# The feed-forwards' matrix products by one level of Strassen's algorithm, with sums of weight blocks made on chip

## The chip, the cores and the metric

The kernel runs on one core of a Trainium2 chip. The core has five engines with a queue each, which wait for one another by semaphores: TensorE (PE in the profile; its weight loads are PEld), VectorE (DVE), ScalarE (ACT), GpSimd (POOL) and SyncE (SP, which issues most transfers). The metric is the time of one execution on the device in microseconds (us), the median of several runs.

## The reference, cut to what matters

The program is a chain of three transformer-like layers on 512 tokens of 1024 features in float32: a gated recurrence, a dilated attention, and a block of sparse attention beside linear attention. Each is followed by a norm and a gated feed-forward of inner width 2816. The change touches the three feed-forwards alone.

```python
def rmsnorm(x, gain):
    xf = x.astype(jnp.float32)
    y = xf * lax.rsqrt(jnp.mean(xf * xf, axis=-1, keepdims=True) + NORM_EPS)
    return (y * gain.astype(jnp.float32)).astype(x.dtype)

def swiglu_ffn(u, w_in, w_down):                 # [512, 1024], [1024, 5632], [2816, 1024]
    gate, up = jnp.split(u @ w_in, 2, axis=-1)
    return (jax.nn.silu(gate) * up) @ w_down

    # first_block, per layer; second block likewise with w_ffn_gate, w_ffn_up, w_ffn_down
    h = h + mix
    h = h + swiglu_ffn(rmsnorm(h, norm_ffn[layer]), ffn_w_in[layer], ffn_w_down[layer])
```

## The kernel before

Activations lie feature-major: a tile is 128 features by 512 tokens. A product of 128 x 128 weights with such a tile is done in three passes (mm3): each operand is split into a head, rounded to the type that PE reads at full pace (fp32r), and a rest, and rest times head, head times head and head times rest are summed in a PSUM bank. So one block of weights costs three matmuls of 512 columns.

The class Weights streams the weights in the order of use. A unit is 1024 columns, that is eight blocks. SP loads it (w_raw, three buffers), ACT casts it to the head (w_hi), and DVE for even units, POOL for odd ones, subtracts the head from the raw weights (w_lo, the rest). `take` hands out blocks; after 3/8 of a unit it has the heads of up to three units made, after 5/8 the rests. Nothing else decides the order there: each engine runs its instructions in the order in which this code issues them, and a tile that is not there makes the whole queue of its reader wait.

A feed-forward (ffn) runs in two halves of 11 inner tiles. For each inner tile, gemm makes the gate and the up product over 8 blocks each (evac_up: DVE scales the gate by the norm's factor r_bc, ACT applies silu, POOL multiplies by r_bc, DVE multiplies with the up product, then h is split into its parts by ACT and DVE). Then the half's 8 output tiles are made over 11 blocks each and added to the residual x (evac_dn), in the second half with the operands and squares of the next norm (norm_feed). The first operands u are x times the gain, split; the norm's factor is applied after the product, since it is known only two tiles later. In the last feed-forward, finish makes the last output tile in two halves of the tokens, so that the first half can be normed and stored under the second.

All operations are recorded by a wrapper, so nearly every row of the profile has line L228; in the changed kernel that line is L263. Rows are told apart by the names of their tiles: ps is a PSUM bank, u and h are the operands' parts.

Of the kernel before, what the change touches and what calls it, by code (L numbers as in the profile page):

```python
# [17 lines left out]
KD = 8  # L18
FF = 22
FH = 11  # L20
# [4 lines left out]
# columns of the packed per-feature vectors  # L25
# [10 lines left out]
# columns of the constants that stay  # L36
# [16 lines left out]
def nsa_rows():  # L53
    """Feature order of the NSA heads: tile j holds head j of group 0 and head j of group 1."""
    return np.concatenate([np.arange((e * 4 + j) * 64, (e * 4 + j) * 64 + 64) for j in range(4) for e in range(2)])


def attn_heads():
    """(head of the group, group) in the order in which the output projection takes them."""
    return [(t, g) for t in range(4) for g in (1, 2)] + [(t, 0) for t in range(4)]  # L60


def weight_plan():
    """The order in which weight blocks are used: (section, [(matrix, k tile, columns)])."""
# [14 lines left out]
    def ffn(name_in, name_down, name_up=None):  # L79
        out = []  # L80
        for half in range(2):
            tiles = []
            for i in range(FH):
                tiles.append(cols((half * FH + i) * 128))
                tiles.append(cols(FF * 128 + (half * FH + i) * 128))
            out += fm(name_in, range(KD), tiles, 2 if half == 0 else 1)
            out += fm(name_down, range(half * FH, half * FH + FH), [cols(m * 128) for m in range(8)], 2)
        return out
# [9 lines left out]
    plan.append(("hgrn", c))  # L98
# [8 lines left out]
    plan.append(("attn", c))  # L107
# [26 lines left out]
    plan.append(("blk2", c))  # L134
    plan.append(("ffn2", ffn("fin2", "fdn2")))
# [3 lines left out]
def plan_units(sec, chunks):  # L139
    """Cut a section's blocks into units of at most UNIT columns; the first ones are small, to start early."""  # L140
# [171 lines left out]
class Program:  # L312
# [1144 lines left out]
    def finish(self, hh):  # L1457
# [41 lines left out]
        for k in range(FH):  # L1499
            product(0, k)  # L1500
# [151 lines left out]
```

## Time and profile before

| | |
|---|---|
| median of 3 runs | 2164.24 us (2163.97 to 2165.24) |
| profiled execution: span from first to last instruction | 2162.1 us |
| PE busy | 2117.4 us, 98% |
| DVE, ACT, POOL busy | 1004.3, 783.8, 723.6 us |
| weights read, mean rate over the span | 187.25 MB read from HBM, 88 GB/s |
| mean granted PE clock | 0.994 |

The profiled execution has no time of its own beside its span; the median of the runs is 2.1 us above that. Busy times are unions over the span; a matmul's recorded duration includes its way through the array, so the pace is read from the distance between starts. The engines beside PE are less busy, but each stage has its own share, so stages are read in windows.

### The profile page before, as it was taken

How to read it: one execution, taken by the hardware profiler on the slowest of the kernel's cores; microseconds unless marked ns; L12 is line 12 of the kernel's file. 1: busy time of each engine (PE TensorE's matmuls, PEld its weight loads, DVE VectorE, ACT ScalarE, POOL GpSimd, SP SyncE). 2: the span in 40 equal slices, each digit the busy share in tenths (PEclk: the TensorE clock that was granted, in tenths of full speed). 3: DMA queues.
4: the chain of work that ended last, by engine and by line, in shares of the span. 5: the costliest groups of instructions: out<-in, count | busy, mean ns of one | idle time of the engine just before them, and what ended most of it. 6: DMA issues, size and time to landing. Idle time of an engine off the chain costs nothing.

```text
span 2162.1 us, 25412 instructions
## 1 busy us (share of the span) xinstructions
PE 2117.4 (98%) x9983; PEld 1773.4 (82%) x9983; DVE 1004.3 (46%) x1775; ACT 783.8 (36%) x1290; POOL 723.6 (33%) x442
## 2 busy tenths in 40 slices
PE   9999999999999999999999999999899999999998
PEld 7787788888888998788888888887688788888887
DVE  4778853322334555643322333447778753222322
ACT  5343443222233433443222224244455543222233
POOL 4413343323333434323322335331511253322333
PEclk9999999999999999999999999999999999999999
DMA  5111233323323222222332232321111223333332
GB/s 178 59 59 49 69 127 98 98 98 98 98 88 107 79 88 78 79 69 98 98 102 93 98 98 92 133 69 48 55 55 57 70 95 98 98 98 98 96 100 69
DMA packets 55865, 191.00 MB, mean 88 GB/s; under 512 B 6257, under 2 KB 8321, under 8 KB 55745
## 3 DMA queue, kind: packets, MB, share of 16 engines
q1 hardware_dynamic: 53584, 183.85, 26.2%
q0 software_dynamic: 1008, 3.42, 0.4%
q10 hardware_dynamic: 1152, 2.10, 0.3%
q8 instruction: 78, 1.28, 0.2%
q14 instruction: 43, 0.34, 0.1%
HBM read 187.25 MB, written 2.10 MB: 88 GB/s over the span
## 4 chain that ended last, share of the span: by engine, by line
PE 86%; DVE 9%; issue 1%; POOL 1%; ACT 1%; DMA 1%; SPq 0%; DVEq 0%; ACTq 0%; POOLq 0%
PE ps L228 86%; DVE Q L228 2%; DVE Sd L228 2%; DVE P L228 1%; DMA w_raw<-in_hgrn 1%; DVE w_lo L228 1%; DVE K L228 0%; POOL rot L228 0%; DVE Pc L228 0%; DVE qs L228 0%; POOL rs L228 0%; DVE obl L228 0%; DVE GQ L228 0%; DVE PT L228 0%; POOL w_lo L228 0%
## 5 line engine op out<-in xcount | busy, mean ns | idle before, releaser
L228 PE MATMUL ps<-u,w_hi 128*128 128x512 f32 x3392 | 1049.4, 391 | 0.0
L228 PEld LDWEIGHTS ps<-u,w_hi 128*128 128x128 f32 x3392 | 638.9, 188 | 128.9 <-issue 1.4
L228 PE MATMUL ps<-u,w_lo 128*128 128x512 f32 x1696 | 683.7, 403 | 2.2 <-POOL w_lo L228 2.2
L228 POOL TENSOR_TENSOR w_lo<-w_raw,w_hi 128x1024 fp32r<-128x1024 f32 (+2 forms) x173 | 415.8, 2403 | 745.1 <-ACT w_hi L228 636.2
L228 ACT CAST w_hi<-w_raw 128x1024 fp32r<-128x1024 f32 (+2 forms) x346 | 356.1, 1030 | 301.6 <-PE ps L228 205.4
L228 PEld LDWEIGHTS ps<-u,w_lo 128*128 128x128 f32 x1696 | 319.7, 189 | 68.3 <-issue 4.2
L228 PE MATMUL ps<-h,w_hi 128*128 128x512 f32 (+1 forms) x1078 | 326.3, 385 | 0.0
L228 DVE TENSOR_TENSOR w_lo<-w_raw,w_hi 128x1024 fp32r<-128x1024 f32 (+2 forms) x173 | 231.5, 1338 | 183.7 <-ACT w_hi L228 175.4
L228 PEld LDWEIGHTS ps<-h,w_hi 128*128 128x128 f32 x1078 | 200.9, 188 | 40.4
L228 PE MATMUL ps<-h,w_lo 128*128 128x512 f32 (+1 forms) x539 | 207.6, 385 | 0.5 <-DVE x L228 0.5
L228 POOL TENSOR_TENSOR sg<-sg,r_bc 128x512 f32<-128x512 f32 x66 | 85.8, 1299 | 290.3 <-ACT sg L228 290.3
L228 DVE TENSOR_TENSOR x<-x,ps 128x512 f32<-128x512 f32 (+1 forms) x73 | 49.5, 678 | 218.6 <-PE ps L228 218.6
L228 PE MATMUL ps<-w_hi,u 128*128 128x512 f32 (+1 forms) x448 | 139.1, 392 | 2.3 <-DVE u L228 2.3
L228 DVE TENSOR_TENSOR h<-ps,sg 128x512 f32<-128x512 f32 x66 | 45.7, 692 | 194.9 <-PE ps L228 182.4
L228 ACT ACTIVATE sg<-gs 128x512 f32<-128x512 f32 x66 | 41.7, 632 | 242.3 <-DVE gs L228 242.3
L228 ACT CAST h<-h 128x512 fp32r<-128x512 f32 x66 | 41.0, 620 | 242.8 <-DVE h L228 242.8
L228 DVE TENSOR_TENSOR gs<-ps,r_bc 128x512 f32<-128x512 f32 x66 | 45.6, 691 | 156.8 <-PE ps L228 156.7
L228 PEld LDWEIGHTS ps<-h,w_lo 128*128 128x128 f32 x539 | 101.2, 188 | 20.9 <-DVE x L228 0.7
L228 ACT ACTIVATE P<-P,nm 128x128 f32<-128x128 f32 (+2 forms) x112 | 55.2, 494 | 142.6 <-DVE nm L228 130.4
L228 POOL TENSOR_TENSOR sq_acc<-sq_acc,sq 128x512 f32<-128x512 f32 x48 | 67.2, 1405 | 117.8 <-ACT sq L228 115.7
L228 PEld LDWEIGHTS ps<-w_hi,u 128*128 128x128 f32 x448 | 95.0, 226 | 10.3 <-DVE u L228 2.7
L228 PE MATMUL ps<-w_lo,u 128*128 128x512 f32 (+1 forms) x224 | 85.8, 383 | 0.0
(294 smaller groups left out, 2231.5 us busy)
## 6 DMA issues: line engine op xcount, KB each, us to landing
w_raw<-in_ffn SPq DMA_DIRECT2D x198, 512.0 KB, 3.5
w_raw<-in_attn SPq DMA_DIRECT2D x48, 512.0 KB, 3.5
w_raw<-in_blk SPq DMA_DIRECT2D x47, 512.0 KB, 3.4
w_raw<-in_hgrn SPq DMA_DIRECT2D x36, 512.0 KB, 3.5
w_raw<-in_blk SPq DMA_DIRECT2D x7, 404.0 KB, 2.9
x<-in_xt SPq DMA_DIRECT2D x8, 256.0 KB, 5.1
w_raw<-in_hgrn SPq DMA_DIRECT2D x8, 256.0 KB, 4.0
x<-in_xt ACTq DMA_DIRECT2D x8, 256.0 KB, 5.0
```

The costliest lines, as they stand in the source:

```text
L228: r = f(*args, **kw)
```

## The change

Where the diff takes comments and docstrings away, nothing changes. What it does:

- **Strassen's form.** The product of a pair of weight tiles (gate and up tile of one inner index, or two output tiles) with an even number of inner blocks and 512 tokens is cut in two along each of the three dimensions. Seven products of half size replace eight; in the code they are a1, b1, a2, b2, c, a3, a4, which collect in three banks (a, b and c). Each product's matmuls have 256 columns; the inner dimension of a group is four pairs of blocks for up groups, three or two pairs for down groups. Each of the 22 inner tiles but the first four makes an up group, and the 11 pairs of inner tiles are worked off in chunks of 3, 3, 2 and 3, with four down groups each (three and a plain product in the last feed-forward).
- **Sums of weights.** Four of the seven products need sums of weight quarters. POOL makes them (ws) from the raw tiles, ahead of the heads. Heads of the sums and the raw quarters are cast by ACT in halves of a unit; in this part all rests (w_lo) are made by DVE.
- **Sums of operands.** The norm's factor must be in the operands now, so the normed operands are made anew (normed) beside plain tiles 4 to 7 of the first four inner tiles; POOL makes their sums, ACT the heads (P1, P2, P3), DVE the rests. The inner tiles h are treated in the same way in a4 of each up group: operands_1 for even ones, operands_2 for odd ones.
- **Evacuation.** Each product's part of a bank is evacuated by itself, 256 columns: by an ACT copy the first time, else by DVE additions or a multiplication; POOL multiplies the up half with the silu.
- **Buffers.** Four w_raw buffers, not three; 28 larger tiles, not 26.

By the program's order, matmuls of 512 columns go from 8059 to 3916 and those of 256 columns from 130 to 7381; the other forms stay.

```diff
+FC = 4
+FCHUNKS = [(0, 1, 2), (3, 4, 5), (6, 7), (8, 9, 10)]
+def ffn_jobs(last):
+    ks = [(2 * j, 2 * j + 1) for j in range(KD // 2)]
+    def ups(a, b):
+        return [("u", i, ks) for i in range(a, b)]
+    def downs(c, n=4):
+        return [("d", i, [(2 * q, 2 * q + 1) for q in FCHUNKS[c]]) for i in range(n)]
+    return ups(FC, 7) + downs(0) + ups(7, 13) + downs(1) + ups(13, FF) + downs(2) + downs(3, 3 if last else 4)
+S_AT = {"a1": 0, "b1": 1, "a2": 3, "b2": 4, "c": 5, "a3": 6, "a4": 9}
+S_LAST = {"a1": 0, "b1": 1, "a2": 3, "c": 4, "a3": 5, "b2": 6, "a4": 7}
+def strassen_order(n):
+    at = [(7 * g + t, g, p) for g in range(n) for p, t in (S_AT if g < n - 1 else S_LAST).items()]
+    return [(g, p) for _, g, p in sorted(at)]
...
+    RAW, SPLIT = 4, 3
...
+    def load(self, n):
+        while self.n_dma < min(n, len(self.raws)):
+            r = self.raws[self.n_dma]
+            r[3] = self.raw_p.tile([128, UNIT], F32, name="w_raw", tag="w_raw")
+            self.nc.sync.dma_start(r[3][:, :r[1]], r[0])
+            self.n_dma += 1
...
+    def used(self, i):
+        self.raws[i][2] -= 1
+        self.n_free += self.raws[i][2] == 0
...
+    def quarter(self, grp, q):
+        n = grp["n"]
+        r = self.raw(grp["r"][0 if q[1] == "1" and q != "A21" or q == "A12" else 1])
+        o = 0 if q in ("A11", "A22") else n
+        return r[:, o:o + n]
+    def sums(self, n):
+        while self.n_sum < min(n, len(self.units)):
+            for part in self.units[self.n_sum]:
+                if part[0] == "s" and part[2] in ("b1", "a2", "b2", "a3"):
+                    grp, p = part[1:]
+                    s = grp["s"][p] = self.s2("ws")[:, 0:grp["n"]]
+                    q, ss = (lambda name: self.quarter(grp, name)), grp["s"]
+                    if p == "b1":
+                        self.g.tensor_add(s, q("A21"), q("A22"))
+                    elif p == "a2":
+                        self.g.tensor_sub(s, ss["b1"], q("A11"))
+                    elif p == "b2":
+                        self.g.tensor_sub(s, q("A12"), ss["a2"])
+                    else:
+                        self.g.tensor_sub(s, q("A11"), q("A21"))
+                    for i in {"b1": (1,), "a2": (0,), "b2": (0,), "a3": (0, 1)}[p]:
+                        self.used(grp["r"][i])
+            self.n_sum += 1
+    def source(self, part):
+        if part[0] == "c":
+            return self.raw(part[1])[:, :self.raws[part[1]][1]]
+        grp, p = part[1:]
+        return self.quarter(grp, {"a1": "A11", "c": "A12", "a4": "A22"}[p]) if p in ("a1", "c", "a4") else grp["s"][p]
+    def width(self, part):
+        return self.raws[part[1]][1] if part[0] == "c" else part[1]["n"]
     def heads(self, look):
         while self.n_head < min(self.at + look, len(self.units)):
             u = self.n_head
-            self.load(u + 1)
-            w = self.units[u][2]
+            self.sums(u + 2)
             hi = self.sp_p.tile([128, UNIT], F32R, name="w_hi", tag="w_hi")
             lo = self.sp_p.tile([128, UNIT], F32R, name="w_lo", tag="w_lo")
-            self.a.copy(hi[:, :w], self.raw[u][:, :w])
+            o = 0
+            for part in self.units[u]:
+                w = self.width(part)
+                self.a.copy(hi[:, o:o + w], self.source(part))
+                o += w
             self.split[u] = (hi, lo)
             self.n_head += 1
     def rests(self):
         while self.n_rest < self.n_head:
-            u = self.n_rest
-            w = self.units[u][2]
+            u, o = self.n_rest, 0
             hi, lo = self.split[u]
-            (self.g if u % 2 else self.v).tensor_sub(lo[:, :w], self.raw.pop(u)[:, :w], hi[:, :w].bitcast(F32))
+            for part in self.units[u]:
+                w = self.width(part)
...
+                e = self.g if part[0] == "c" and u % 2 else self.v
+                e.tensor_sub(lo[:, o:o + w], self.source(part), hi[:, o:o + w].bitcast(F32))
+                o += w
+                if part[0] == "c":
+                    self.used(part[1])
+                elif part[2] in ("a1", "c", "a4"):
+                    self.used(part[1]["r"][part[2] == "a4"])
             self.n_rest += 1
-        self.load(self.n_rest + self.RAW - 1)
...
+    def product(self, p):
+        self.begin()
+        unit = self.units[self.at]
+        part = unit[self.idx]
+        assert part[0] == "s" and part[2] == p, (self.at, self.idx, part, p)
+        self.todo = (self.at, self.idx, len(unit))
+        return self.next(part[1]["n"], len(unit))
+    def prepare(self):
+        at, idx, n = self.todo
+        if idx == 0:
+            self.split_from(at)
+        if idx == n - 1:
+            self.rests()
+    def split_from(self, at):
+        now, self.at = self.at, at
+        self.heads(self.look)
+        self.at = now
...
+    def operands_1(self, E1, B12=False):
+        v, a, g = self.v, self.a, self.g
+        g.tensor_sub(E1[:, 2], E1[:, 1], E1[:, 0])
+        P = self.s4("P1", (128, 2, 2, 256), F32R)
+        a.copy(P[:, 0], E1[:, 0::2])
+        v.tensor_sub(P[:, 1], E1[:, 0::2], P[:, 0].bitcast(F32))
+        return {"a1": (P[:, 0, 0], P[:, 1, 0]), "b1": (P[:, 0, 1], P[:, 1, 1])}
+    def operands_2(self, E1, E2):
+        v, a, g = self.v, self.a, self.g
+        g.tensor_sub(E2[:, 2], E2[:, 1], E1[:, 2])
+        g.tensor_sub(E2[:, 3], E2[:, 0], E2[:, 2])
+        hi, lo = (self.s4("P2", (128, 4, 256), F32R) for _ in range(2))
+        a.copy(hi, E2)
+        v.tensor_sub(lo, E2, hi.bitcast(F32))
+        g.tensor_sub(E1[:, 3], E2[:, 1], E1[:, 1])
+        X = {p: (hi[:, i], lo[:, i]) for i, p in enumerate(("c", "b2", "a2", "a4"))}
+        X["a3"] = self.half(E1[:, 3], "P3")
+        return X
+    def half(self, src, name):
+        P = self.s2(name, (128, 2, 256), F32R)
+        self.a.copy(P[:, 0], src)
+        self.v.tensor_sub(P[:, 1], src, P[:, 0].bitcast(F32))
+        return P[:, 0], P[:, 1]
+    def strassen(self, groups):
+        banks = {}
+        for g, p in strassen_order(len(groups)):
+            operands, after = groups[g]
+            key = g, p[0]
+            first = key not in banks
+            if first:
+                banks[key] = self.ps((128, 256))
+            ps, X = banks[key], operands()
+            hi, lo = self.W.product(p)
+            for j in range(len(X)):
+                x, sl = X[j][p], slice(128 * j, 128 * j + 128)
+                self.mm3(ps, (hi[:, sl], lo[:, sl]), x, first and j == 0, j == len(X) - 1)
+            after[p](ps)
+            self.W.prepare()
...
     def ffn(self, gain_name, pre=None, gain=None, operands=True, residues=False):
         v, a, g = self.v, self.a, self.g
...
+        last = not operands
+        n1, n2 = slice(0, 256), slice(256, 512)
+        inner = self.V[self.ffn_gain]
+        E, H, U, sr = {}, {}, [], {}
+        def room(i):
+            if i not in E:
+                E[i] = self.s4("E", (128, 4, 256))
+            return E[i]
+        def normed(j):
+            e = [self.s4("E", (128, 4, 256)) for _ in range(2)]
+            for i in range(2):
+                k = 2 * j + i
+                v.scalar_tensor_tensor(
+                    e[i][:, 0:2].rearrange("p a n -> p (a n)"), self.x[k], inner[:, k:k + 1], self.r_bc, op0=ALU.mult, op1=ALU.mult)
+            X = self.operands_1(e[0])
+            X.update(self.operands_2(*e))
+            U.append(X)
+        def evac_up(i, ps):
+            if i % 2 == 0:
+                gs, sg = self.s2("gs"), self.s2("sg")
+                v.tensor_mul(gs, ps, self.r_bc)
+                a.activation(sg, gs, AF.Silu)
+                g.tensor_mul(sg, sg, self.r_bc)
+                sr[i // 2] = sg
+            else:
+                v.tensor_mul(room(i // 2)[:, 0:2].rearrange("p a n -> p (a n)"), ps, sr.pop(i // 2))
+            if 3 <= i <= 6:
+                normed(i - 3)
+        self.gemm(self.u, 2 * FC, evac_up, lead=2)
+        late = [lambda i=i: inner_operands(i) for i in range(FC)]
+        def inner_operands(i):
+            if i % 2 == 0:
+                H[i // 2] = self.operands_1(E[i])
+            else:
+                H[i // 2].update(self.operands_2(E[i - 1], E[i]))
+                if last and i // 2 in FCHUNKS[-1]:
+                    H[i // 2]["B12"] = self.half(E[i - 1][:, 1], "P3")
+        def up(i):
+            e, t = room(i), self.s2("G")
+            def c(ps):
+                v.tensor_add(t[:, n1], t[:, n1], ps)
+                a.activation(t, t, AF.Silu)
+            def a3(ps):
+                v.tensor_add(e[:, 1], e[:, 1], ps)
+                g.tensor_mul(e[:, 1], e[:, 1], t[:, n2])
+            def a4(ps):
+                v.tensor_mul(e[:, 0], ps, t[:, n1])
+                inner_operands(i)
+            def b2(ps):
+                v.tensor_add(t[:, n2], t[:, n2], ps)
+                for _ in late[:2]:
+                    late.pop(0)()
+            return {
+                "a1": lambda ps: a.copy(t[:, n1], ps), "b1": lambda ps: a.copy(e[:, 1], ps),
+                "a2": lambda ps: a.copy(t[:, n2], ps), "b2": b2, "c": c, "a3": a3, "a4": a4,
+            }
+        def down(i, final):
+            m = 2 * i
+            x1, x2 = self.x[m], self.x[m + 1]
+            left = {"b2", "c"}
+            def add(x, sl, p=None):
+                def f(ps):
+                    v.tensor_add(x[:, sl], x[:, sl], ps)
+                    left.discard(p)
+                    if final and p and not left:
+                        self.norm_feed(m)
+                return f
+            def a4(ps):
+                v.tensor_add(x2[:, n1], x2[:, n1], ps)
+                if final:
+                    self.norm_feed(m + 1)
+            return {
+                "a1": add(x1, n1), "b1": add(x2, n2), "a2": add(x1, n2), "b2": add(x1, n2, "b2"), "c": add(x1, n1, "c"),
+                "a3": add(x2, n2), "a4": a4,
+            }
...
+        for n, (what, i, pairs) in enumerate(ffn_jobs(last)):
+            if what == "u":
+                groups.append((lambda: U, lazy(n, lambda i=i: up(i))))
+                continue
+            qs = [k // 2 for k, _ in pairs]
+            final = qs[-1] == FCHUNKS[-1][-1]
...
+            def make(i=i, final=final):
+                if final and i == 0:
+                    begin_norm()
+                return down(i, final)
+            groups.append((lambda qs=qs: [H[q] for q in qs], lazy(n, make)))
+        self.strassen(groups)
         if last:
-            self.finish(hh)
+            self.finish([z for q in FCHUNKS[-1] for z in ([H[q]["a1"], H[q]["B12"]], [H[q]["c"], H[q]["b2"]])])
```

On DVE, in the middle of the first feed-forward, this stood before: h is the gated inner tile, gs the scaled gate, x the residual.

```order
L228 TENSOR_TENSOR w_lo<-w_raw,w_hi 128x1024
L228 TENSOR_TENSOR gs<-ps,r_bc 128x512
L228 TENSOR_TENSOR h<-ps,sg 128x512
L228 TENSOR_TENSOR h<-h 128x512
L228 TENSOR_TENSOR w_lo<-w_raw,w_hi 128x1024 x2
L228 TENSOR_TENSOR x<-x,ps 128x512 x3
L228 TENSOR_TENSOR w_lo<-w_raw,w_hi 128x1024
```

In the changed kernel DVE has these rows around the end of an odd up group: the evacuation of a3 (E), two rests of weights, the evacuation of a4, the rests of the pair's operands (P_5571 is P2, P_5575 is P3), then the rests for c and a3 of the next group, its b2 evacuation (G) and the rests for the group after.

```order
L263 TENSOR_TENSOR E<-E,ps 128x256
L263 TENSOR_TENSOR w_lo<-ws,w_hi 128x512 x2
L263 TENSOR_TENSOR E<-ps,G 128x256
L263 TENSOR_TENSOR P_5571<-E,P_5570 128x1024
L263 TENSOR_TENSOR P_5575<-E,P_5575 128x256
L263 TENSOR_TENSOR w_lo<-w_raw,w_hi 128x512
L263 TENSOR_TENSOR w_lo<-ws,w_hi 128x512
L263 TENSOR_TENSOR G<-G,ps 128x256
L263 TENSOR_TENSOR w_lo<-w_raw,w_hi 128x512
L263 TENSOR_TENSOR w_lo<-ws,w_hi 128x512
```

What moved: between a PSUM evacuation and the next weights' rests there now stand the operands' rests, which wait for POOL and ACT; the weights' rests are in pieces of 512 columns and all on this queue.

On POOL, at the end of the first half's up tiles, this stood before: the odd units' rests between multiplications by r_bc.

```order
L228 TENSOR_TENSOR w_lo<-w_raw,w_hi 128x1024
L228 TENSOR_TENSOR sg<-sg,r_bc 128x512
L228 TENSOR_TENSOR w_lo<-w_raw,w_hi 128x1024 x7
L228 TENSOR_TENSOR sg<-sg,r_bc 128x512
L228 TENSOR_TENSOR w_lo<-w_raw,w_hi 128x1024
```

In the changed kernel POOL has these rows in the same odd up group: the product of silu and up half, the sums a3 and (of the next group but one) b1, three sums of operands, the sums a2 and b2, and the next group's.

```order
L263 TENSOR_TENSOR E<-E,G 128x256
L263 TENSOR_TENSOR ws<-w_raw 128x512 x2
L263 TENSOR_TENSOR E<-E 128x256 x3
L263 TENSOR_TENSOR ws<-ws,w_raw 128x512
L263 TENSOR_TENSOR ws<-w_raw,ws 128x512
L263 TENSOR_TENSOR E<-E,G 128x256
L263 TENSOR_TENSOR ws<-w_raw 128x512
L263 TENSOR_TENSOR E<-E 128x256
```

What moved: POOL has no rests of weights here any more; each up group puts four sums of 512 columns on it, and the sums of operands, of which the second waits for DVE's evacuation of a4, stand behind two of them.

## Rows read from the trace of the kernel before

**Rows 1.** The page: busy time, share, instructions; then the chain by engine and line.

```profile
PE 2117.4 (98%) x9983; PEld 1773.4 (82%) x9983; DVE 1004.3 (46%) x1775; ACT 783.8 (36%) x1290; POOL 723.6 (33%) x442
...
PE ps L228 86%; DVE Q L228 2%; DVE Sd L228 2%; DVE P L228 1%; DMA w_raw<-in_hgrn 1%; DVE w_lo L228 1%; DVE K L228 0%; POOL rot L228 0%; DVE Pc L228 0%; DVE qs L228 0%; POOL rs L228 0%; DVE obl L228 0%; DVE GQ L228 0%; DVE PT L228 0%; POOL w_lo L228 0%
```

**Rows 2.** Windows, first feed-forward: busy PE, PEld, DVE, ACT, POOL (instructions), clock, DMA, GB/s.

```profile
319.00:679.00 360.00, 360.00 (x1594) 297.96 (x1593) 111.10 (x127) 104.84 (x129) 118.22 (x63) 1.00 0.30 97
```

**Rows 3.** Timeline of PE in the last feed-forward: start us, us, engine, line, operation, shapes.

```profile
2135.37 0.39 PE L228 MATMUL ps<-h,w_lo 128*128 128x512 f32 x1
...
2136.05 0.39 PE L228 MATMUL ps<-h,w_lo 128*128 128x512 f32 x1
...
2142.52 0.28 PE L228 MATMUL ps<-h,w_lo 128*128 128x256 f32 x1
...
2142.88 0.28 PE L228 MATMUL ps<-h,w_lo 128*128 128x256 f32 x1
```

**Rows 4.** Timeline of DVE near the first feed-forward; in brackets, what ended the idle time.

```profile
308.32 0.68 DVE L228 TENSOR_TENSOR x<-x,ps 128x512 f32<-128x512 f32 x1
309.79 2.71 DVE L228 SCALAR_TENSOR_TENSOR u<-x,vec,u 128x512 fp32r<-128x512 f32 x1 [0.79 <-ACT u L228]
312.42 2.30 DVE L228 TENSOR_TENSOR w_lo<-w_raw,w_hi 128x1024 fp32r<-128x1024 f32 x1
...
341.27 0.69 DVE L228 TENSOR_TENSOR h<-h 128x512 fp32r<-128x512 f32 x1 [0.69 <-ACT h L228]
...
346.01 1.50 DVE L228 TENSOR_TENSOR h<-h 128x512 fp32r<-128x512 f32 x1 [0.69 <-ACT h L228]
...
355.19 1.23 DVE L228 TENSOR_TENSOR w_lo<-w_raw,w_hi 128x1024 fp32r<-128x1024 f32 x1 [0.26 <-ACT w_hi L228]
```

**Rows 5.** Groups of equal instructions: count, busy us, mean ns of one, idle before.

```profile
L228 ACT CAST w_hi<-w_raw 128x1024 fp32r<-128x1024 f32 x329 | 343.1, 1044 | 277.0 <-PE ps L228 185.3 <-issue 55.4 <-DVE x L228 13.0
...
L228 ACT CAST h<-h 128x512 fp32r<-128x512 f32 x66 | 41.0, 620 | 242.8 <-DVE h L228 242.8
...
L228 DVE TENSOR_TENSOR K<-K,KT 128x384 f32<-128x384 f32 x24 | 13.1, 547 | 0.0
...
L228 DVE TENSOR_TENSOR GK<-GK,T 128x256 f32<-128x256 f32 x12 | 5.1, 426 | 0.4
...
L228 POOL TENSOR_TENSOR KT<-KT,F 128x256 f32<-128x256 f32 x4 | 4.4, 1107 | 0.3
...
L228 DVE TENSOR_TENSOR out<-x,ps 128x256 f32<-128x256 f32 x12 | 4.2, 414 | 2.5 <-ACT r_bc L228 2.5
```

**Rows 6.** Timeline of POOL in the same stretch as rows 4.

```profile
308.28 1.30 POOL L228 TENSOR_TENSOR sq_acc<-sq_acc,sq 128x512 f32<-128x512 f32 x1 [3.10 <-ACT sq L228]
309.53 2.42 POOL L228 TENSOR_TENSOR w_lo<-w_raw,w_hi 128x1024 fp32r<-128x1024 f32 x1
311.89 1.76 POOL L228 TENSOR_TENSOR sq_acc<-sq_acc,sq 128x512 f32<-128x512 f32 x1
...
344.55 2.42 POOL L228 TENSOR_TENSOR w_lo<-w_raw,w_hi 128x1024 fp32r<-128x1024 f32 x1
```

**Rows 7.** Timeline where a product ends: PE's next matmul and DVE's evacuation.

```profile
678.99 0.39 PE L228 MATMUL ps<-u,w_lo 128*128 128x512 f32 x1
...
679.19 0.69 DVE L228 TENSOR_TENSOR x<-x,ps 128x512 f32<-128x512 f32 x1 [2.99 <-PE ps L228]
```

**Rows 8.** DMA issues of the feed-forwards' weights: count, KB each, median us to landing.

```profile
w_raw<-in_ffn SPq DMA_DIRECT2D x198, 512.0 KB, 3.5
```

**Rows 9.** PE after an idle time, then windows: busy us by engine, granted clock (PEclk).

```profile
181.06 1.16 PE L228 MATMUL ps<-Q,K 128*128 128x192 f32 x3 [2.11 <-DVE Q L228]
...
178.00:181.00 3.00, 0.95 (x5) 0.45 (x3) 2.96 (x5) 0.00 (x0) 1.51 (x1) 1.00 0.08 19
181.21:184.62 3.41, 3.41 (x11) 3.12 (x12) 3.27 (x10) 0.00 (x0) 0.00 (x0) 0.50 0.30 120
```

More of the change, by code (lines that the diff above doesn't have):

```diff
@@ L19 @@
 FF = 22
-FH = 11
 NEG = -1e30
@@ L77, in cols, with ffn @@
         return np.arange(o, o + n)
[L79 to L87, printed above, removed]
+    def ffn(name_in, name_down, last=False):
+        up = [(cols(i * 128), cols((FF + i) * 128)) for i in range(FF)]
+        first = fm(name_in, range(KD), [c for t in up[:FC] for c in t], 2)
+        groups = []
+        for what, i, pairs in ffn_jobs(last):
+            if what == "u":
+                groups.append((name_in, pairs, *up[i]))
+            else:
+                groups.append((name_down, pairs, cols(2 * i * 128), cols((2 * i + 1) * 128)))
+        out = [("c", first), ("s", groups)]
+        if last:
+            ks = [k for q in FCHUNKS[-1] for k in (2 * q, 2 * q + 1)]
+            out.append(("c", fm(name_down, ks, [cols(m * 128) for m in (6, 7)])))
         return out
@@ L297, in take, with next @@
                 self.rests()
+    def next(self, n, count):
+        hi, lo = self.split[self.at]
+        r = hi[:, self.pos:self.pos + n], lo[:, self.pos:self.pos + n]
+        self.idx += 1
+        self.pos += n
+        if self.idx == count:
+            self.at, self.idx, self.pos = self.at + 1, 0, 0
+        return r
+    def take(self, n):
+        self.begin()
+        _, _, widths = self.units[self.at][0]
         if self.idx == 3 * len(widths) // 8:
@@ new lines, in ffn, with lazy, step, f @@
+        groups, made = [], {}
+        def lazy(key, make):
+            def step(p):
+                def f(ps):
+                    if key not in made:
+                        made[key] = make()
+                    made[key][p](ps)
+                return f
+            return {p: step(p) for p in S_AT}
+        def begin_norm():
+            self.norm_begin(self.V[gain_name] if gain_name else gain, pre=pre, operands=operands, residues=residues)
+        for n, (what, i, pairs) in enumerate(ffn_jobs(last)):
+            if what == "u":
+                groups.append((lambda: U, lazy(n, lambda i=i: up(i))))
+                continue
+            qs = [k // 2 for k, _ in pairs]
[5 more added lines that the diff above has]
+            groups.append((lambda qs=qs: [H[q] for q in qs], lazy(n, make)))
@@ L1459, in finish @@
         v, a, g = self.v, self.a, self.g
+        K = len(hh)
+        parts = [slice(0, 256), slice(256, 512)]
+        ps, w6 = self.ps(), [self.W.take(128) for _ in range(K)]
+        for p in range(2):
+            for k in range(K):
+                self.mm3(ps[:, parts[p]], w6[k], hh[k][p], k == 0 and p == 0, k == K - 1)
+        a.activation(self.sm("warm", (128, 1)), self.eps, AF.Sqrt)
+        v.tensor_add(self.x[KD - 2], self.x[KD - 2], ps)
+        self.norm_feed(KD - 2)
         x, sq, ps, w = self.x[KD - 1], self.s2("sq"), self.ps(), []
-        parts = [slice(0, 256), slice(256, 512)]
         def product(p, k):
@@ L1523, in run @@
         self.hgrn()
+        self.ffn_gain = "ffn0"
         self.ffn("mix1", residues=True)
```

119 lines of the change are left out of this document (53 added, 66 removed).

## The prediction

> **What bounds the kernel now.** I read the page first: TensorE (PE) is busy 2117.4 of 2162.1 us, and 86% of the chain that ended last lies on its matmuls [rows 1]. Then the stretch of the first feed-forward: PE is busy in all of its 360 us, DVE in 111, POOL in 118 [rows 2]. So its time is the matmuls' pitch. Then matmul starts: one block in three passes (rest, head, head) takes 0.68 us at 512 columns (2135.37 to 2136.05) and 0.36 us at 256 (2142.52 to 2142.88) [rows 3]. A half-size matmul thus costs 53% of a full one, not 50%. A feed-forward has 528 such triples: 359 us, which agrees with rows 2.
>
> **What the change takes from PE.** By the program's order 4143 matmuls of 512 columns go and 7251 of 256 come. 4143 × 0.2267 − 7251 × 0.12 = 69 us less, if PE stays the bound. In the unit used below: an up group (one gate and one up tile) was 16 triples of 0.68 = 10.88 us and becomes 28 of 0.36 = 10.08 us, 1.44 us a product; two groups 21.76 and 20.16.
>
> **What it adds beside PE.** Durations for operations alone, two inputs in SBUF: DVE 0.69 us at 512 columns and 1.23 at 1024 (341.27, 355.19) [rows 4], 0.55 at 384 and 0.43 at 256 [rows 5]; POOL 1.30 and 2.42 (308.28, 309.53) [rows 6], by the straight line between them 1.02 at 384 and 0.74 at 256 (ends: half of 1.30, and the 1.11 of one with strides [rows 5]). A DVE evacuation of 256 columns from PSUM takes 0.41, ACT's casts of 1024 and 512 take 1.04 and 0.62 [rows 5].
>
> The question is whether DVE and POOL run side by side. The traced overlaps say no [rows 4, 6], where both of DVE's inputs lie in SBUF. The h subtraction, 0.69 alone, took 1.50 beside POOL's w_lo of 344.55 to 346.97. At 309.53 POOL's w_lo starts; DVE's u of 309.79 ends only at 312.50, 0.55 after it; POOL's sq_acc then ends 1.15 after u (313.65), and DVE's w_lo 1.07 after that (314.72). Each waits for the other to finish and then needs its own duration less 0.14 us, so I charge this shared port 0.55 (DVE 512), 1.07 (1024), 0.41 (384), 0.28 (256), and POOL 1.15, 0.88, 0.60. An addition with one input in PSUM is free of it: x at 308.32 took 0.68 under POOL's sq_acc.
>
> The Trainium skill (SBUF — State Buffer, Who interferes with whom) says that whoever comes second is blocked until the first has finished. If whole durations are charged, as that reads, two up groups need 26.9 us of the port; by the rows it is 22.4.
>
> **Up groups, 54 of them.** DVE per two groups: 14 rests of 512, P1 (512), P2 (1024), P3 (256): 14 × 0.55 + 0.55 + 1.07 + 0.28 = 9.6 us of port. POOL: 8 sums of 512 and 6 operations of 256: 9.2 + 3.6 = 12.8. Together 22.4, already above 21.76. And the queues are in order, so I lay out one pair by hand from the order rows of the section on the change. An evacuation starts 0.2 us after PE's next product (679.19 against 678.99) [rows 7].
> - After an odd group's a4 product, the evacuation ends at 0.6 us. POOL can't follow: before E it holds a product, a3's sum and the next b1's sum. With DVE's two rests between them these are 0.60 + 0.55 + 0.55 + 1.15 + 1.15 = 4.0 us from 2.1 us before a4's end, when a3's evacuation is done: to 1.9. Two E operations: 3.2. ACT's cast: 4.3. P2's rest waits for POOL's last E and the a2 sum, until 5.0, and takes to 6.1; POOL's b2 sum 7.2; P3's rest 7.5; only then the rest of c's weights, 8.1. PE, after a2 and b2, wanted c at 2.9. It stands 5.3 us.
> - After an even group's a4: evacuation 0.6, E 1.35, cast 2.0, P1's rest behind POOL's b1 sum 3.1, a2's sum 4.25, a3's weights 4.8; PE wanted them at 4.3. That and the next product's weights behind the b2 sum cost 0.8 us.
>
> A pair takes 20.16 + 5.3 + 0.8 = 26.3, which is 4.5 more than before; 27 pairs: **+123 us**. The end below is the port's 22.4 (+17 us). The end above is 26.9 (nothing of two operations overlaps) with 1.5 us of low clock (last rival): 28.4, +179. I take the laid-out pair, as the waits in it come from the order itself.
>
> **Front of the Strassen part.** Tiles 4 to 7 of the plain product (21.76 us of PE) get the making of eight normed operands beside them. Port, to the first product's last operand: POOL 13 E operations of 0.60, two sg 1.15, two w_lo 2.28 and three sums 1.15 = 18.1; DVE eight normings and four P1 0.55, three P2 1.07, three P3 0.28, one w_lo 1.07, two 0.55 = 12.8. 30.9 − 21.8 = 9.1 of standing, and more where a chain leaves the port idle: I take 11, three times: **+33**. Ends 0 (DVE's own work fits) and 16 each. The four tiles made in that product get their operands in the first pair of up groups: 8.6 us of port, of which 26.3 − 22.4 = 3.9 finds room: 4.7 each, **+14**; ends 0 and 26.
>
> **Down groups.** Before: 12 triples (three pairs) 8.16 us, 8 triples 5.44. Now PE needs 7.56 and 5.04. DVE starts an operation some 0.07 us before the last one's end (312.42 against 312.50) and has 7 rests and 7 evacuations: 7 × (0.48 + 0.35) = 5.8, and POOL's four sums 3.5 of port beside them. Of the 24 plain groups of three I expect 8.2, **0**; ends 7.56 and 9.4 (every sum blocks): −14, +31. The 12 groups of two: DVE 5.0 and sums of 2.4, so 6.2: **+9**; ends −5, +24. Final groups also make the next norm's operands, two subtractions on DVE (0.55 of port each), and POOL adds squares (1.15 each): port 7 × 0.41 + 4 × 0.88 + 2 × 0.55 + 2 × 1.15 = 9.8 in the first feed-forward, 12.1 in the second (two sets of squares), 8.7 in the three groups of the last (no subtraction). With some slack 10.2, 12.2 and 8.7: 4 × 2.0 + 4 × 4.0 + 3 × 0.5 = **+26**; ends 0, +45. The last tile's inner dimension is 6 blocks, not 11, so less lies over the first half's norm: **+1**, ends 0, +3.
>
> The same weight bytes are read, in smaller pieces of the same order; a transfer lands in 3.5 us [rows 8]. The b1 sum's second buffer is asked for when a4's rest frees it, some 3.6 us before POOL wants it: just hidden, and 0.3 us a pair if not. The other sections hold the same operations as before: 0.
>
> Sum: 123 + 33 + 14 + 0 + 9 + 26 + 1 = 206. Profiled span 2162.1 + 206 = 2368; the median of the runs, 2164.2, is 2.1 above that span, so **2370 us**.
>
> **Rivals.**
> - PE stays the bound: 2162.1 − 69 + 2.1 = 2095. For it: before, both helpers are a third busy [rows 2]. Against it: the port alone wants 22.4 in a pair, and without any port the odd chain (0.6 + 0.74 + 1.04 + 1.16 + 0.36 + 0.62 = 4.5 us against PE's 2.9) gives 20.16 + 1.6 = 21.8, no gain. By the Trainium skill's gap between matmuls (TensorE: Matmul & The Clock Gate, Back-to-back issue gap: columns at 2.4 GHz plus 2.5 ns) the 69 would be an estimate of 102 us, and the time 2062; rows 3 show 226.7 and 120 ns where it gives 215.7 and 109.
> - Only the port counts, since POOL runs ahead and the waits fall together: pairs of 22.4. 17 + 27 + 26 + 0 + 9 + 23 + 1 = 103: 2267. Decides if P2's rest waits under 2 us. For it: up to six products' sums are made ahead. Against it: rests are made only two or three products ahead, behind P2's on the same queue.
> - The clock falls as well. After 2.11 us of idle PE ran a stretch of 3.41 us at a granted 0.50, that is at 1.2 GHz [rows 9]; a stand of 5.3 us in each pair would bring that back 27 times, at 1.7 us each: +46, 2416.
>
> **Chances and range.** The laid-out pair 0.51, with 2300 to 2400 as its own range; clock as well 0.22; port only 0.17; PE the bound 0.09, since the rows hold stretches of some us and not a whole stage in which both queues are full; past all of these 0.01. The lower ends together give 2162, the upper 2520; 8 in 10 lie in 2220 to 2470. A measurement of this kernel tells 0.2% from no change. Only the PE case and the lower ends of the port case can be at or under that: faster 0.09, same 0.02, slower 0.89.
>
> **What would show it.** PE's busy share falls under 92%, with idle before c's first matmul ended by DVE's w_lo; DVE's w_lo of 512 columns average 1.0 us or more, not 0.69; POOL's sums over 1.4; 24 to 28 us between two odd groups' P2. Wrong if those w_lo stay at 0.69 beside POOL's sums, or PE shows no idle in up groups; the size is wrong if pairs take 22 or 29 us.

## The result, and the profile after

The changed kernel takes 2466.1 us (2464.8 to 2468.3), against 2164.7 us before: ratio 1.1396 (95% interval 1.138 to 1.1412). Forecast were 2370 us in a range of 2220 to 2470. The direction and the mechanism hold; the loss is 301 us and not 206, and the time lies 4 us under the upper end of the range.

The page of the changed kernel, busy times and the chain by engine and by line, beside [rows 1]:

```profile
PE 2166.8 (88%) x13091; PEld 1950.4 (79%) x13091; DVE 1683.2 (68%) x2883; ACT 1056.6 (43%) x2056; POOL 1191.2 (48%) x940
...
PE 15%; DVE 7%; POOL 5%; issue 3%; ACT 2%; DMA 1%; DVEq 0%; POOLq 0%; ACTq 0%
```

PE is busy for 88% of the span, down from 98%, though it holds less work: its 2166.8 us contain matmuls at half clock. The chain that ended last covers only a third of the span here; PE has 15 of its 33%, where it had 86 of 99% before, and transfers have 1%.

The windows of the changed kernel: the first feed-forward, then three stretches in and behind a stand in it (busy us of PE, PEld, DVE, ACT, POOL with instructions; granted clock; DMA share; GB/s), beside [rows 2]:

```profile
316.30:778.60 462.30, 379.63 (x2638) 360.42 (x2636) 336.61 (x497) 195.24 (x385) 276.50 (x228) 0.90 0.23 74
...
656.87:662.15 5.28, 5.04 (x23) 5.04 (x24) 2.74 (x6) 1.62 (x3) 0.00 (x0) 0.50 0.35 102
649.72:656.87 7.15, 1.84 (x16) 1.64 (x14) 3.69 (x3) 2.74 (x6) 6.30 (x6) 0.92 0.00 0
663.64:671.00 7.36, 7.36 (x64) 7.36 (x62) 5.59 (x7) 4.42 (x10) 5.65 (x5) 1.00 0.44 142
```

The first feed-forward went from 360 to 462 us. In the third row PE runs b2 and then stands while POOL works; in the second it runs c and most of a3 at a granted 0.50, that is at 1.2 GHz, for 5.28 us; the fourth, in the group after it, is at full clock.

One such stand in the timeline, the one place on which the forecast's largest term rested: PE, then POOL, ACT and DVE (start us, us; in brackets the idle time before and what ended it), beside [rows 4, 6, 7]:

```profile
622.63 0.40 PE L263 MATMUL ps<-P,w_hi 128*128 128x256 f32 x2
628.61 0.58 PE L263 MATMUL ps<-P,w_lo 128*128 128x256 f32 x1 [5.59 <-DVE w_lo L263]
628.99 0.63 PE L263 MATMUL ps<-P,w_hi 128*128 128x256 f32 x2
629.42 0.41 PE L263 MATMUL ps<-P,w_lo 128*128 128x256 f32 x1
```

```profile
617.86 1.06 POOL L263 TENSOR_TENSOR E<-E,G 128x256 f32<-128x256 f32 x1 [2.89 <-DVE E L263]
618.88 3.18 POOL L263 TENSOR_TENSOR ws<-w_raw 128x512 f32<-128x512 f32 x2
622.02 2.23 POOL L263 TENSOR_TENSOR E<-E 128x256 f32<-128x256 f32 x3
624.21 1.27 POOL L263 TENSOR_TENSOR ws<-ws,w_raw 128x512 f32<-128x512 f32 x1
625.56 2.12 POOL L263 TENSOR_TENSOR ws<-w_raw,ws 128x512 f32<-128x512 f32 x1
```

```profile
623.60 1.35 ACT L263 CAST P<-E 128x1024 fp32r<-128x1024 f32 x2 [2.32 <-POOL E L263]
```

```profile
620.19 0.42 DVE L263 TENSOR_TENSOR E<-ps,G 128x256 f32<-128x256 f32 x1 [0.72 <-PE ps L263]
624.68 3.28 DVE L263 TENSOR_TENSOR P<-E,P 128x1024 fp32r<-128x1024 f32 x2 [4.07 <-ACT P L263]
627.88 0.68 DVE L263 TENSOR_TENSOR w_lo<-w_raw,w_hi 128x512 fp32r<-128x512 f32 x1
```

Read it from the end. PE waits 5.59 us for c's w_lo (627.88). It stands behind P2's and P3's rests (624.68), these behind ACT's cast (623.60), this behind POOL's E (622.02), and E behind one product and two sums of weights that POOL began at 617.86. Counted from the end of the odd group's a4 (619.99), POOL came to E at 2.0, P2's rest began at 4.7, c's rest was done at 8.6; forecast were 1.9, 5.0 and 8.1, and a stand of 5.3. Behind it two matmuls take 0.43 us (628.99 to 629.42), not 0.24.

Groups of equal instructions in the changed kernel (count, busy us, mean ns of one, idle before), beside [rows 5]:

```profile
L263 DVE TENSOR_TENSOR w_lo<-ws,w_hi 128x512 fp32r<-128x512 f32 x216 | 222.5, 1043 | 6.4 <-ACT w_hi L263 5.6
...
L263 DVE TENSOR_TENSOR P<-E,P 128x1024 fp32r<-128x1024 f32 x45 | 79.1, 1757 | 122.7 <-ACT P L263 122.6
...
L263 DVE TENSOR_TENSOR P<-E,P 128x256 fp32r<-128x256 f32 x48 | 59.6, 1246 | 0.0
```

The means are 1.04, 1.76 and 1.25 us; alone the three take 0.69, 1.23 and 0.43. (The rests of raw quarters of 512 columns take 0.90.)

**Where the 302.7 us of the profiled span lie.** By the starts of every product's first matmul, the Strassen parts take 1211.6 us; their work before took 1380 triples × 0.68 = 938.4. So +273. PE's own stream would be 7245 × 0.12 = 869.4 (−69, as forecast). Of these matmuls 809 begin while the granted clock is 0.50; from start to start they are then 0.21 us apart and not 0.12, which makes 74: the low clock. What is left, 268, is standing, short waits between matmuls included. The fronts add 30.1 (44.5 us each before; 55.0, 53.6 and 55.0 now); the rest of the kernel gives back 0.6.

### The profile page after: what moved, and what is told of

It reads as the page before. It is cut to its first block, busy times and chain, and to the rows that moved or that the text cites. A ratio compares the mean times of both kernels' runs of the same rounds, so it can differ in the third digit from the quotient of the medians.

```text
span 2464.8 us, 34738 instructions
## 1 busy us (share of the span) xinstructions
PE 2166.8 (88%) x13091; PEld 1950.4 (79%) x13091; DVE 1683.2 (68%) x2883; ACT 1056.6 (43%) x2056; POOL 1191.2 (48%) x940
## 5 line engine op out<-in xcount | busy, mean ns | idle before, releaser
L263 PE MATMUL ps<-P,w_hi 128*128 128x256 f32 x4878 | 952.9, 297 | 0.0
L263 PE MATMUL ps<-P,w_lo 128*128 128x256 f32 x2439 | 745.4, 306 | 234.5 <-DVE w_lo L263 212.3
L263 PEld LDWEIGHTS ps<-P,w_hi 128*128 128x128 f32 x4878 | 821.2, 207 | 0.7 <-DVE P L263 0.7
L263 PEld LDWEIGHTS ps<-P,w_lo 128*128 128x128 f32 x2439 | 504.2, 207 | 264.6 <-DVE w_lo L263 207.0
L263 PE MATMUL ps<-u,w_hi 128*128 128x512 f32 x1664 | 520.4, 394 | 0.0
L263 DVE TENSOR_TENSOR w_lo<-w_raw,w_hi 128x512 fp32r<-128x512 f32 (+3 forms) x390 | 368.0, 944 | 91.3 <-ACT w_hi L263 83.7
L263 ACT CAST w_hi<-w_raw 128x512 fp32r<-128x512 f32 (+4 forms) x477 | 343.7, 722 | 152.6 <-PE ps L263 109.8
L263 PE MATMUL ps<-u,w_lo 128*128 128x512 f32 x832 | 349.8, 420 | 19.4 <-POOL w_lo L263 14.6
L263 PEld LDWEIGHTS ps<-u,w_hi 128*128 128x128 f32 x1664 | 316.2, 190 | 62.5 <-issue 1.4
L263 DVE TENSOR_TENSOR w_lo<-ws,w_hi 128x512 fp32r<-128x512 f32 (+2 forms) x404 | 352.6, 884 | 12.5 <-ACT w_hi L263 10.9
L263 POOL TENSOR_TENSOR E<-E,G 128x256 f32<-128x256 f32 x54 | 55.3, 1024 | 235.6 <-DVE E L263 190.5
```

What stands on the lines that cost most here:

```text
L263: r = f(*args, **kw)
```

## The experiments

Edits are against the changed kernel unless said otherwise. Times are medians, ratios against the kernel before on the same chip with their 95% interval. "Standing" and "low clock" are worked out as above. A pair is the time of the 14 products of an even and an odd up group, each from its start to the next product's, on the mean of the 21 pairs from tile 8 on (28.64 us in the changed kernel, 21.76 before).

| | time, us | ratio | standing | low clock | pair |
|---|---|---|---|---|---|
| changed kernel | 2466.1 | 1.1396 (1.138 to 1.1412) | 268 | 74 | 28.64 |
| operands late | 2413.1 | 1.1155 (1.112 to 1.119) | 232 | 53 | 26.16 |
| sums on DVE | 2379.7 | 1.1001 (1.0945 to 1.1057) | 207 | 44 | 24.41 |
| both | 2318.1 | 1.0716 (1.0685 to 1.0747) | 172 | 21 | 22.10 |
| no weight sums | 2264.0 | 1.0464 (1.0407 to 1.0522) | 112 | 37 | 23.15 |
| no operand sums | 2291.2 | 1.059 (1.0559 to 1.0621) | 159 | 35 | 24.33 |
| no sums | 2133.9 | 0.9868 (0.9839 to 0.9896) | 38 | 1 | 20.46 |

**The order on DVE's queue.**

```diff
                 v.tensor_mul(e[:, 0], ps, t[:, n1])
-                inner_operands(i)
+                self.pend.append(lambda: inner_operands(i))
...
             after[p](ps)
             self.W.prepare()
+            while self.pend:
+                self.pend.pop(0)()
```

> Edit: in each up group of the changed kernel the operands of the inner tile (POOL's E, ACT's cast, DVE's rests P1, P2, P3) are issued one step later, behind the heads and rests of the weights that are issued at the same place; nothing is added or left out. My theory (DVE's queue is in order, and c's weights stand behind P2's rest, which waits for POOL): the 4.6 us before an even group's c go, to under 0.5, and part of it comes back later, about 2.4 us before the odd group's a1, because DVE's next weights' rests now stand behind P2; a steady pair of up groups falls from 28.6 to 23.4 to 25 us, the whole to about 2350 us (2320 to 2390). Rival (the shared port's load alone sets the pair, order doesn't matter): pair 28 or more, whole within 1% of 2466. Rival (POOL's length of queue): the wait stays before c since sums for c's neighbours come late, whole 2440 or more.

The stand before an even c is gone, and PE waits elsewhere. PE's matmuls after an idle time, 31 us of steady up groups:

```profile
588.63 0.39 PE L263 MATMUL ps<-P,w_lo 128*128 128x256 f32 x1 [1.19 <-ACT G L263]
...
592.33 0.39 PE L263 MATMUL ps<-P,w_lo 128*128 128x256 f32 x1 [2.01 <-DVE w_lo L263]
...
604.17 0.36 PE L263 MATMUL ps<-P,w_lo 128*128 128x256 f32 x1 [2.54 <-DVE w_lo L263]
...
619.20 0.39 PE L263 MATMUL ps<-P,w_lo 128*128 128x256 f32 x1 [1.79 <-DVE w_lo L263]
```

So the order made that stand. But only 53 us came back, not 75 to 145: the pair is 26.2, above the 23.4 to 25 expected. Of the new waits the one before the odd group's a1 was laid out (592.33 and 619.20: 2.0 and 1.8 us); the one before its a3 (604.17: 2.5 us), behind the next rests on the same queue, was not, nor the one before its even group's a3 (588.63: 1.2 us). Both rivals fall (a pair of 28 or more, the whole at 2440 or more).

**Sums on DVE.**

```diff
-                        self.g.tensor_add(s, q("A21"), q("A22"))
+                        self.v.tensor_add(s, q("A21"), q("A22"))
                     elif p == "a2":
-                        self.g.tensor_sub(s, ss["b1"], q("A11"))
+                        self.v.tensor_sub(s, ss["b1"], q("A11"))
...
```

> Edit: the changed kernel with the eight sums of weight quarters of each pair of up groups (and those of the down groups) on DVE in place of POOL; order of issue as it was. Theory of the shared port and of POOL's queue ahead of E: DVE's rests of 512 columns go back from 1.04 us to about 0.7, E is no longer behind two sums of 1.3 us on POOL, so the stand before c shrinks from 4.6 to about 3.5 us at worst (P2's rest and two sums are still ahead of c's rest on DVE); pair 24 to 26.5 us, whole about 2390 us (2340 to 2420). Rival (DVE and POOL work side by side, and DVE is the late one): DVE gets 5.5 us more in a pair, pair 30 or more, whole over 2490.

2380, and the pair 24.4. The same groups as above, in this run, with the sums now on DVE:

```profile
L263 DVE TENSOR_TENSOR w_lo<-ws,w_hi 128x512 fp32r<-128x512 f32 x216 | 180.0, 843 | 0.0
...
L263 DVE TENSOR_TENSOR P<-E,P 128x1024 fp32r<-128x1024 f32 x45 | 55.5, 1233 | 74.4 <-ACT P L263 74.4
...
L263 DVE TENSOR_TENSOR P<-E,P 128x256 fp32r<-128x256 f32 x48 | 21.4, 451 | 0.0
```

P2's and P3's rests are back at 1.23 and 0.45 us, the weights' rests at 0.84, not at the 0.7 expected. Three pairs (the same six groups) in the changed kernel and in this run:

```profile
586.15:673.33 87.18, 68.46 (x507) 67.05 (x506) 59.50 (x73) 37.23 (x75) 53.69 (x43) 0.88 0.22 73
...
571.87:643.32 71.45, 63.50 (x506) 62.27 (x505) 58.86 (x97) 37.44 (x75) 15.41 (x18) 0.98 0.25 89
```

DVE has eight instructions more in a pair and is no busier: 19.6 us of 23.8, against 19.8 of 29.1 in the changed kernel. Its 19.8 were to a good part waiting for POOL inside instructions. This is the strongest sign for the port: if the two worked side by side, 5.5 us more would have stood here. The 86 us that the run gains aren't the port's alone, since E also stands behind two sums less on POOL.

**Both.** The two edits together.

> Edit: both of the former, the later operands and the sums of weights on DVE. By the theory DVE has some 18 us in a pair and the port under 18, PE 20.2, and c's rest no longer stands behind P2: pair 20.2 to 21.5 us, no idle over 1 us in steady up groups, clock at 2.4 GHz there, whole about 2240 us (2190 to 2280), still above 2164 by the front, the late operands and the last down groups. Rival (DVE too full, 22 instructions over 20 us with their waits): pair 23 to 25, whole 2300 to 2370.

2318, inside the rival's 2300 to 2370 and above the 2190 to 2280 of the theory; the pair of 22.1 lies between the two (20.2 to 21.5, and 23 to 25). In three steady pairs:

```profile
562.41:628.25 65.84, 62.83 (x506) 60.99 (x505) 61.18 (x97) 37.36 (x75) 17.40 (x18) 1.00 0.28 97
```

PE is at full clock and stands only 3 us of 66; DVE is busy in 61.2 of 65.8, 20.4 us a pair where I had reckoned with 18. The pair of 22.1 is DVE's queue. The other half of the miss lies outside steady pairs: the fronts (28.6 us) and the first four tiles' late operands kept their waits, and groups of three pairs take 8.88 us, not 8.27.

**The port by itself**, in the kernel before:

```diff
                     hh[i // 2] = self.split(h, "h")
+                dum = self.s2("dum")
+                for _ in range(2):
+                    g.tensor_add(dum, self.cst[:, 0:512], self.cst[:, 0:512])
```

> Edit: the kernel before, with two additions of 128x512 (both inputs in SBUF, output read by nobody) added on POOL after each of the 132 up-tile evacuations. PE, DVE, ACT and their order stay as they are, and POOL gets 2.6 us more in each 5.44 us, so no queue is over full. Theory of the shared port: DVE's operations with two inputs in SBUF get longer with nothing changed on DVE: w_lo of 1024 columns from 1.40 us to 1.7 or more in the first feed-forward, the h subtraction of 512 from 0.73 to 1.0 or more; those with an input in PSUM (gs, h from ps) stay at 0.69. Whole 2164 to 2175 us, since PE bounds. Rival (DVE and POOL share nothing; what was long in the changed kernel was something else): w_lo and h stay within 0.1 us.

The groups of DVE and POOL in the first feed-forward of this run:

```profile
L228 POOL TENSOR_TENSOR dum<-cst 128x512 f32<-128x512 f32 x88 | 120.0, 1370 | 3.5
...
L228 DVE TENSOR_TENSOR w_lo<-w_raw,w_hi 128x1024 fp32r<-128x1024 f32 x32 | 51.7, 1614 | 39.3 <-ACT w_hi L228 38.4
...
L228 DVE TENSOR_TENSOR h<-h 128x512 fp32r<-128x512 f32 x22 | 17.7, 803 | 15.1 <-ACT h L228 15.1
L228 DVE TENSOR_TENSOR h<-ps,sg 128x512 f32<-128x512 f32 x22 | 15.2, 692 | 68.8 <-PE ps L228 64.0 <-POOL sg L228 4.8
L228 DVE TENSOR_TENSOR gs<-ps,r_bc 128x512 f32<-128x512 f32 x22 | 15.2, 690 | 47.2 <-PE ps L228 47.1
```

w_lo went from 1.40 to 1.61 us and h from 0.73 to 0.80, in the expected direction but less than expected; those that read PSUM stayed at 0.69. The means move little, since the operations that meet one of POOL are only some more than before (of 1024 columns some 85 of 167, where it was some 55). Sorted one by one (over the whole run), a DVE operation of 512 columns with both inputs in SBUF that starts inside a POOL operation ends 0.55 us after that one's end (median of some 60), one of 1024 columns 1.08 after it; in the changed kernel the medians are 0.55 (over 200 such operations, which take 1.4 us on the mean) and 1.08. These are the charges of the forecast, 0.55 and 1.07. By the Trainium skill (SBUF — State Buffer, Who interferes with whom) a DVE instruction with two SBUF inputs contends with a GpSimd instruction that reads SBUF, and the port pair that they share is an exclusive lock: the trace agrees, but for 0.14 us that overlap. The whole took 2179 us (ratio 1.0076, 1.0047 to 1.0105), 4 more than I had allowed: PE now waits for POOL's w_lo, 11.2 us in the whole run where it was 2.2.

**The clock.** Forty matmuls of 256 columns without a reader in the stand before c of each even up group but the first:

```diff
             if first:
-                banks[key] = self.ps((128, 256))
+                bank = self.ps()
+                banks[key] = bank[:, 0:256]
+                if p == "c" and g and evens[g]:
+                    x = groups[g][0]()[0]
+                    for _ in range(40):
+                        self.mm(bank[:, 256:512], x["a1"][0][:, 0:128], x["c"][0])
```

> Edit: in the changed kernel PE runs 40 more matmuls of 256 columns, of resident operands into an unused half of c's bank, between b2 and c of each even up group but the first: 24 places of about 4.4 us in a stand of 4.6; nothing waits for their output. Theory (the clock falls because PE stands): c, a3 and a1 behind the stand run at 2.4 GHz, 2.07 us a pair come back, 24 times: -50 us, whole about 2416 (2405 to 2430), and the mean clock rises from 0.944 to 0.96 or more. Rival (the clock falls for another reason, such as the mix of matmuls): the low clock stays, whole 2460 or more, higher by what of the dummies doesn't fit the stand.

2430.5 (ratio 1.1236, 1.1203 to 1.1268). PE's timeline around one filled stand, and the windows of the c and a3 behind two of them:

```profile
643.68 4.96 PE L263 MATMUL ps<-P,P 128*128 128x256 f32 x40
649.55 0.39 PE L263 MATMUL ps<-P,w_lo 128*128 128x256 f32 x1 [0.91 <-DVE w_lo L263]
```

```profile
621.91:627.19 5.28, 5.03 (x42) 5.03 (x43) 4.49 (x9) 2.08 (x5) 1.30 (x2) 1.00 0.33 99
649.31:652.45 3.14, 2.90 (x24) 2.90 (x25) 2.65 (x6) 0.45 (x1) 0.00 (x0) 1.00 0.39 151
```

The clock stays at 1.00 behind the filled stand, so the standing brings it down, not the mix of matmuls. Low clock fell from 74 to 28 us (−46, near the 50 expected), in the 21 steady pairs from 38 to nothing. The time fell only by 36: the standing, dummies counted in, grew from 268 to 278. The dummies don't hold c up, which still waits 0.91 us for its w_lo. The likely reading is that POOL and DVE catch up while PE runs at half pace, so that about a fifth of the low clock's time had been paid for by shorter waits.

**The sums left out.** Both kinds, then each alone:

```diff
-            self.sums(u + 2)
...
-        return self.quarter(grp, {"a1": "A11", "c": "A12", "a4": "A22"}[p]) if p in ("a1", "c", "a4") else grp["s"][p]
+        return self.quarter(grp, {"a1": "A11", "c": "A12", "a4": "A22", "b1": "A21", "a2": "A11", "b2": "A12", "a3": "A11"}[p])
...
-        g.tensor_sub(E1[:, 2], E1[:, 1], E1[:, 0])
...
-        a.copy(P[:, 0], E1[:, 0::2])
+        a.copy(P[:, 0], E1[:, 0:2])
```

> Edit: the changed kernel with all of Strassen's sums left out, those of weights (each product takes a raw quarter) and those of operands on POOL (E); P2's cast and rest have 512 columns in place of 1024. All 256-column matmuls, casts, weights' rests and evacuations stay, so PE's stream is the same but the numbers are not Strassen's. Theory (the sums, on the port and in the queues, cost the time, not the matmuls): a steady pair of up groups at 20.2 to 20.8 us, PE at 2.4 GHz, whole 2100 us (2085 to 2130), some 65 under the kernel before. Rival (matmuls of 256 columns with twice the weight loads, or the clock in such a mix, cost it): whole over 2160.

Three steady pairs of it:

```profile
522.40:583.68 61.28, 61.24 (x506) 60.63 (x505) 43.31 (x77) 36.62 (x77) 6.63 (x6) 1.00 0.31 104
```

PE is busy throughout and a pair takes 20.4: the 256-column stream is as cheap as read from [rows 3], and the front is back at 44.5. At 2134 us it gains 28 us, not the 69 of PE's stream; I had expected 2100. Of the some 40 us between, 26 lie in the final down groups (9.9 us each, where PE needs 7.56), in which the next norm's operands are made.

> Edit: the changed kernel with the sums of weights left out alone (each product takes a raw quarter); the sums of operands on POOL and everything else stay, in the old order. Theory: E is no longer behind POOL's weight sums, but c's rest is still behind P2's: after an odd group's a4, evacuation 0.6, two E operations to 2.1, cast to 3.1, P2's rest to 4.3, P3's to 4.7, c's to 5.3, PE wants it at 2.9: 2.4 us of standing, with a clock that falls less; pair 22.6 to 24.5 us, whole about 2310 us (2270 to 2350). Rival (weight sums are the whole cost, operand sums none): pair under 21, whole under 2200.

> Edit: the changed kernel with the sums of operands left out alone (P1 and P2 of 512 columns, from the tiles themselves); the sums of weights on POOL stay. Theory: the port has 18 us in a pair, under PE's 20.2; after an odd a4 no E stands between, only P2's and P3's rests, which each meet a weight sum once: c's rest at about 4.7, PE wants it at 2.9; pair 21.5 to 23 us, whole about 2280 us (2240 to 2320). Rival (the weight sums alone fill the port or POOL's queue): pair over 25, whole over 2370.

Without weight sums 202 us go, without operand sums 175, without both 332: each costs, and they cost 45 less together than apart, since some waits go with either. With the operand sums half of P2's cast and rest goes too, so the 175 and the 332 are the price of the sums and of the heads and rests that they need. Times were a little under the range of the first and inside that of the second; the second's pair, 24.3, is above my 21.5 to 23. The chain from a4 to c is too short in my layout again: in a pair of this run (a4's end at 579.08) P2's and P3's rests meet one sum each, and c's rest meets a third (it starts at 583.05, takes 1.74 us and is done at 5.7, not 4.7).

**Sums of down groups back on POOL**, in the kernel with both edits:

```diff
+                    e = self.v if grp["n"] == 512 else self.g
...
-                        self.v.tensor_add(s, q("A21"), q("A22"))
+                        e.tensor_add(s, q("A21"), q("A22"))
```

> Edit: as the run with later operands and sums on DVE, but with the sums of the down groups on POOL again. In that run DVE was the full queue in down groups (three-pair groups 8.88 us against 8.27 with sums on POOL). Theory (each stage has its own scarce one: the port in up groups, DVE's queue in down groups): three-pair groups back to 8.3, final ones to 11.2, whole about 2300 us (2285 to 2312). Rival (the port counts in down groups as well): 8.8 or more, whole 2318 or more.

2331.4 (1.0781, 1.075 to 1.0812): the rival's side. On the mean the second group of a chunk fell from 8.8 us to 8.1, but the first, beside which the moved operands of the last up tile are made, rose from 9.8 to 11.3. Groups of three are 9.04 on the mean, against 8.88: the port counts here as well. In time the down groups come out even (those of three +4 us, the final ones −4, at 11.1 each, 11.2 expected); the 13 us lost lie mostly in the last up group before each chunk (tile 12: 13.4 us, from 11.4), where POOL now makes the first down group's sums.

**A version that beats both** kernels was not found: the best with all its sums is 2318 us, and even with every sum left out 28 us are won. The sums' least price in these versions, 2318 − 2134 = 184 us, is over six times that.

## Why the forecast was right in its direction and short by 96 us

By its own terms, profiled span against span:

| term | forecast | measured |
|---|---|---|
| pairs of up groups, 27 × | +123 (4.5 each) | +186 (6.9 each) |
| late operands of the first four tiles | +14 | +25 |
| fronts | +33 | +30 |
| down groups of three | 0 | +3 |
| down groups of two | +9 | +27 |
| final groups | +26 | +34 |
| tail and the other sections | +1 | −1 |

- **PE's stream** is −69 as worked out; the run without sums comes near it (a steady pair of 20.46 for 20.16).
- **The stand after an odd a4**, from the order of the queues, held: 5.59 us in the stand shown against 5.3, and it goes when that order is changed. Standing in all: the forecast's 173 us in the Strassen parts stand on a stream that is 69 shorter, which makes 242; measured 268.
- **The port** held: the charges are those measured one by one, and moving POOL's sums off it, and out of E's way, gives 86 us.
- **The step that failed is the clock.** "The clock falls as well" stood as a rival at 0.22, with +46, and the likeliest case had it at nothing. It fell: the low clock takes 74 us, by this account three quarters of the 96 that were missing; the rest is standing. A fall after 2.11 us of idle stood in [rows 9], so a stand of 5.3 gave no reason to leave it out. The rival's size for a pair was near: 1.8 us in a steady one, forecast 1.7 (the sum's upper end has 1.5). But the rival counted one such stand in each pair and nothing else, 46 us; the 21 steady pairs have 38 of the 74, tiles 4 to 7 have 20, and down and final groups, which stand too, 16.
- **The rows by place.** A steady pair of 28.64 is PE's 20.16, 6.0 of idle (forecast 6.1), 1.8 of low clock and 0.6 of short waits, which had no term. Late operands were put on one pair, at 4.7; measured they burden the first two pairs, at 4.2 each, clock included. The two-pair groups' +27 is mostly not theirs: the last odd tile's stand falls before the first one's c, 17.9 us of idle over three feed-forwards. The final groups came out at 11.4, 12.4 and 9.3 us, forecast 10.2, 12.2 and 8.7.
- **The rivals.** PE as the bound (2095) falls: DVE and POOL between them have 22 us to do in a pair. The port alone (2267) falls as the changed kernel stands. That its 22.4 us is the floor of a pair with POOL's sums isn't shown: with the order changed the pair came to 26.2, and only with POOL's sums on DVE to 22.1, where DVE's queue takes over.
- **Range and signs.** The laid-out pair's own range of 2300 to 2400 doesn't hold the result. That the wide range does, by 4 us, is luck in part: the likeliest case alone doesn't lead there. Of the signs, PE's share (88%, under 92), c's wait for w_lo and POOL's sums (1.45 to 1.85 us, over 1.4) came; the rests of 512 columns take 0.98 on the mean of both kinds, just under 1.0, and the pair of 28.6 is over the 24 to 28, near the 29 that was to count as wrong.

What stays open is how the 74 would divide into net loss and time that the queues catch up: the filled stands gave back 36 of 46, from 24 places, and the first groups, the downs and the ends weren't filled.

## What to carry to other kernels

Fewer multiplications pay only if their sums have an engine to lie on: here 69 us of PE were to be had, and the sums cost 184 us in the best of the versions tried. Before trading PE's time for DVE's and POOL's, add up what both do with two SBUF inputs as one queue, and lay out one period in the order of issue, for a rest that waits on a long chain holds up every weight behind it. When that layout shows PE standing for 5 us, as here, charge the low clock that follows to the likeliest case, in every stage that has such stands.

## What the hardware showed beyond that

- After a stand of some 5.6 us PE ran 5.28 us at a granted 0.50 in one place, and about 3 us at that pitch in another (628.61 to 631.55); with the stand filled by matmuls that nobody reads the clock stayed at 1.00. Not every shorter stand is followed by it: in the run without operand sums PE ran at a granted 1.00 after one of 2.49 us (561.65), and at 0.50 after one of 2.73 (584.85).
- The low clock's cost isn't wholly lost where the feeding engines are the bound: 46 us less of it gave 36 us.
- A DVE operation with two SBUF inputs that starts inside a POOL operation shows up as a longer DVE operation, not as a wait: DVE "busy" 19.8 us of a pair became 19.6 with eight instructions more.
